# Softmax of 16,384 rows: transfers of 3 to 32 rows per partition in place of transfers of 8

## The chip, the cores and the metric

The kernel runs on one core of a Trainium2 chip. The metric is the device time of one execution, in microseconds (us). The span that the profile shows is about 1.8 us shorter than the device time (161.3 us of span for 163.08 us). All positions in time below are counted from the start of the span. The engines that matter are DVE (VectorE), ACT (ScalarE), SP (SyncE, which only issues the loads) and the core's 16 DMA engines.

With one core, a run is called slow when it is over 1.5% above the fastest of the same kernel, and fast otherwise.

## The reference

```python
# x: 16 x 1024 x 512, float32
x_max = np.max(x, axis=-1, keepdims=True)
exp_x = np.exp(x - x_max)
return exp_x / np.sum(exp_x, axis=-1, keepdims=True)
```

There are 16,384 rows of 512 numbers (2 KB), so each of the 128 partitions gets 128 rows. "One row" below means one row on every partition, which is 262,144 bytes. 33.55 MB come in and 33.55 MB go out.

## The kernel before

The input is cut into 16 chunks of 8 rows. A partition's 8 rows lie next to each other in memory, so one transfer moves 128 pieces of 16 KB. Twelve chunks fit at a time (192 KB per partition). The loads are issued by SP and the stores by ACT's queue.

```python
CHUNKS = [8] * 16
SLOTS = {8: 12}
# ... src[k], dst[k]: chunk k as "(p r) d -> p r d"

    def load(k):
        tiles[k] = data.tile([P, R, d], F32, ..., bufs=SLOTS[R])
        nc.sync.dma_start(out=tiles[k], in_=src[k])
    def rowmax(k):          # DVE, one instruction per chunk
        nc.vector.reduce_max(out=shift[k], in_=tiles[k], axis=AX, negate=True)
    def exps(k):            # ACT, one instruction per row, in place, with the row's sum
        for r in range(R):
            nc.scalar.activation(out=tiles[k][:, r, :], in_=tiles[k][:, r, :],
                                 func=EXP, bias=shift[k][:, r:r+1], ...,
                                 accum_out=sums[k][:, r:r+1])
    def scale(k):           # DVE, in place
        nc.vector.reciprocal(out=recip, in_=sums[k])
        for r in range(R):
            nc.vector.tensor_scalar_mul(out=tiles[k][:, r, :], in0=tiles[k][:, r, :], ...)
    def store(k):
        nc.scalar.dma_start(out=dst[k], in_=tiles[k])

        for k in range(K):
            load(k)
            rowmax(k)
            exps(k)
            if k >= 1:
                scale(k - 1)
                store(k - 1)
        scale(K - 1)
        store(K - 1)
```

Each engine works through its own instructions in this order. DVE's order is therefore: maximum of chunk k, then scaling of chunk k - 1.

Of the kernel before, what the change touches and what calls it, by code (L numbers as in the profile page):

```python
# [1 line left out]

# [4 lines left out]

F32 = mybir.dt.float32
EXP = mybir.ActivationFunctionType.Exp
AX = mybir.AxisListType.X  # L10


CHUNKS = [8] * 16

SLOTS = {8: 12}


@with_exitstack
def kernel(
    ctx: ExitStack,  # L20
    tc: tile.TileContext,
    x: bass.AP,
    out: bass.AP,
):
    nc = tc.nc
    P = nc.NUM_PARTITIONS

    x_flat = x.flatten_outer_dims()
    out_flat = out.flatten_outer_dims()
    n, d = x_flat.shape  # L30
    assert n == P * sum(CHUNKS)


    src, dst, at = [], [], 0
    for R in CHUNKS:
        for flat, views in ((x_flat, src), (out_flat, dst)):
            part = flat[at : at + P * R, :]
            views.append(part.rearrange("(p r) d -> p r d", r=R))
        at += P * R

    data = ctx.enter_context(tc.tile_pool(name="data", bufs=1))
    stats = ctx.enter_context(tc.tile_pool(name="stats", bufs=4))

    K = len(CHUNKS)
    tiles = [None] * K
    shift = [None] * K
    sums = [None] * K

    def load(k):
        R = CHUNKS[k]  # L50
        tiles[k] = data.tile([P, R, d], F32, name=f"x{R}", tag=f"x{R}", bufs=SLOTS[R])
        nc.sync.dma_start(out=tiles[k], in_=src[k])  # L52

    def rowmax(k):
        R = CHUNKS[k]
        shift[k] = stats.tile([P, R], F32, name=f"shift{R}", tag=f"shift{R}")
        nc.vector.reduce_max(out=shift[k], in_=tiles[k], axis=AX, negate=True)  # L57

    def exps(k):
        R = CHUNKS[k]  # L60
        sums[k] = stats.tile([P, R], F32, name=f"sums{R}", tag=f"sums{R}")
        for r in range(R):
            nc.scalar.activation(  # L63
                out=tiles[k][:, r, :],
                in_=tiles[k][:, r, :],
                func=EXP,
                bias=shift[k][:, r : r + 1],
                scale=1.0,
                accum_out=sums[k][:, r : r + 1],
            )  # L70

    def scale(k):
        R = CHUNKS[k]
        recip = stats.tile([P, R], F32, name=f"recip{R}", tag=f"recip{R}")
        nc.vector.reciprocal(out=recip, in_=sums[k])  # L75
        for r in range(R):
            nc.vector.tensor_scalar_mul(  # L77
                out=tiles[k][:, r, :],
                in0=tiles[k][:, r, :],
                scalar1=recip[:, r : r + 1],  # L80
            )

    def store(k):
        nc.scalar.dma_start(out=dst[k], in_=tiles[k])  # L84

    with tc.manual_schedule():
        for k in range(K):
            load(k)
            rowmax(k)
            exps(k)  # L90
            if k >= 1:
                scale(k - 1)
                store(k - 1)
        scale(K - 1)
        store(K - 1)


# [1 line left out]
_INS = ['x']  # L99
_OUTS = [((16, 1024, 512), 'float32')]  # L100


# [23 lines left out]
```

## Time and profile before

| | before |
|---|---|
| device time, median | 163.06 us (162.9 to 163.22) |
| span | 161.3 us |
| DVE busy / ACT busy | 123.8 us / 93.2 us |
| DMA busy, both queues (98.1% of the span) | 158.2 us |
| span less DMA busy | 3.1 us |
| last store issued | 149.49 us |

The lines below are from the page of the kernel before. The rows of DVE and DMA give the busy tenths in 40 slices of the span (about 4 us each). GB/s is what the DMA engines moved. The two queue lines give packets, MB and their time as a share of 16 engines' span (q1 carries the loads, q10 the stores). Then come the chain that ended last, the groups (busy us, mean ns of one, idle time before them) and the transfers (KB each, median us from issue to landing).

```profile
span 161.3 us, 527 instructions
DVE 123.8 (77%) x160; ACT 93.2 (58%) x257; POOL 0.2 (0%) x4
...
DVE  0088799999999999985970079999999999957000
...
DMA  6999999999999999999999999999999999999993
GB/s 163 431 427 427 431 435 378 418 445 431 423 439 431 421 435 431 431 439 418 439 435 427 431 427 435 435 425 435 431 427 439 431 427 427 431 435 431 431 435 171
...
q1 hardware_dynamic: 2304, 33.56, 49.5%
q10 hardware_dynamic: 2304, 33.56, 48.6%
...
DMA 52%; DVE 31%; ACT 6%; SPq 2%; issue 1%; ACTq 1%; DVEq 0%
...
L63 ACT ACTIVATE x<-x,shift 128x512 f32<-128x512 f32 x128 | 90.5, 709 | 44.1 <-DVE shift L57 21.4
L57 DVE TENSOR_REDUCE shift<-x 128x8 f32<-128x4096 f32 x16 | 70.6, 4415 | 9.7 <-DMA x<-in_x_dram 9.7
L77 DVE TENSOR_SCALAR x<-x,recip 128x512 f32<-128x512 f32 x128 | 52.1, 482 | 0.6
...
x<-in_x_dram SPq DMA_DIRECT2D x16, 2048.0 KB, 42.6
out_dram<-x ACTq DMA_DIRECT2D x16, 2048.0 KB, 18.0
```

And from the timeline (start us, us, engine, line, operation), the last store:

```profile
149.49 0.34 ACTq L84 DMA_DIRECT2D out_dram<-x  x1
```

How to read it: the DMA engines are at 90% or more in every slice but the first and the last, at about 431 GB/s, and 49.5% + 48.6% of the span is 158.2 us. DVE and ACT have idle time that costs nothing, because the DMA is the limit. At that rate one row costs the DMA about 0.608 us (262,144 bytes at 431 GB/s), whether it is loaded or stored, so a load or store of 8 rows costs 4.9 us and one of 32 rows 19.5 us. For DVE a row costs 0.97 us: 4415 ns for the maxima of 8, 3.26 us for 8 scalings in the timeline, and a reciprocal.

The rate is what the Trainium skill leads one to expect: "HBM Reference", section "Specifications (TRN2)", says that a core streaming alone measures about 425 GB/s, bounded by its 16 DMA engines. This trace agrees, with 427 to 435 GB/s in most slices.

### The profile page before, as it was taken

What the parts mean: (1) busy time and instruction counts of PE and PEld (TensorE: products, weight loads), DVE (VectorE), ACT (ScalarE), POOL (GpSimd) and SP (SyncE); (2) the same over time, 40 slices, a digit from 0 to 9 for tenths busy, and PEclk for the clock granted to TensorE, in tenths of its full rate; (3) what the DMA queues carried; (4) which work ended last, traced back from release to release, by engine and by line L of the source; (5) the groups of instructions that cost most, each with busy time, mean ns of one, the idle gap of its engine ahead of it and who ended that gap; (6) DMA issues with size and microseconds to landing.
All of it is one profiled execution on the core that took longest, in us unless ns stands there. A gap on an engine that the chain in (4) does not pass through costs nothing.

```text
span 161.3 us, 527 instructions
## 1 busy us (share of the span) xinstructions
DVE 123.8 (77%) x160; ACT 93.2 (58%) x257; POOL 0.2 (0%) x4
## 2 busy tenths in 40 slices
DVE  0088799999999999985970079999999999957000
ACT  0037994959596867067002996859595959591000
POOL 0000000000000000000000000000000000000000
DMA  6999999999999999999999999999999999999993
GB/s 163 431 427 427 431 435 378 418 445 431 423 439 431 421 435 431 431 439 418 439 435 427 431 427 435 435 425 435 431 427 439 431 427 427 431 435 431 431 435 171
DMA packets 4612, 67.14 MB, mean 416 GB/s; under 512 B 513, under 2 KB 513, under 8 KB 513
## 3 DMA queue, kind: packets, MB, share of 16 engines
q1 hardware_dynamic: 2304, 33.56, 49.5%
q10 hardware_dynamic: 2304, 33.56, 48.6%
q14 instruction: 4, 0.02, 0.0%
HBM read 33.55 MB, written 33.55 MB: 416 GB/s over the span
## 4 chain that ended last, share of the span: by engine, by line
DMA 52%; DVE 31%; ACT 6%; SPq 2%; issue 1%; ACTq 1%; DVEq 0%
DMA x<-in_x_dram 52%; DVE shift L57 16%; DVE x L77 14%; ACT x L63 6%; SPq L52 2%; DVE recip L75 1%; ACTq L84 0%; DVEq L121 0%; ACTq L63 0%
## 5 line engine op out<-in xcount | busy, mean ns | idle before, releaser
L63 ACT ACTIVATE x<-x,shift 128x512 f32<-128x512 f32 x128 | 90.5, 709 | 44.1 <-DVE shift L57 21.4
L57 DVE TENSOR_REDUCE shift<-x 128x8 f32<-128x4096 f32 x16 | 70.6, 4415 | 9.7 <-DMA x<-in_x_dram 9.7
L77 DVE TENSOR_SCALAR x<-x,recip 128x512 f32<-128x512 f32 x128 | 52.1, 482 | 0.6
L63 ACT ACTIVATION_READ_ACCUMULATOR x<-x,shift 128x1 f32 x128 | 24.0, 187 | 0.0
L75 DVE RECIPROCAL recip<-sums 128x8 f32<-128x8 f32 x16 | 3.1, 196 | 15.3 <-ACT x L63 15.3
L63 ACT ACT_TABLE_LOAD x1 | 1.3, 1283 | 8.7 <-DMA x<-in_x_dram 8.7
L110 POOL MEMSET const-bfloat16-1.0<- 128x1 bf16 x1 | 0.1, 102 | 0.0
L110 POOL MEMSET const-uint8-127<- 128x1 uint8 x1 | 0.1, 102 | 0.0
L110 POOL MEMSET const-float32-0.0<- 128x1 f32 x1 | 0.1, 99 | 0.2 <-issue 0.2
L110 POOL MEMSET const-float32-1.0<- 128x1 f32 x1 | 0.1, 99 | 0.0
## 6 DMA issues: line engine op xcount, KB each, us to landing
x<-in_x_dram SPq DMA_DIRECT2D x16, 2048.0 KB, 42.6
out_dram<-x ACTq DMA_DIRECT2D x16, 2048.0 KB, 18.0
```

What stands on the lines that cost most here:

```text
L52: nc.sync.dma_start(out=tiles[k], in_=src[k])
L57: nc.vector.reduce_max(out=shift[k], in_=tiles[k], axis=AX, negate=True)
L63: nc.scalar.activation(out=tiles[k][:, r, :], in_=tiles[k][:, r, :], func=EXP, bias=shift[k][:, r : r + 1], scale=1.0, accum_out=sums[k][: ...
L75: nc.vector.reciprocal(out=recip, in_=sums[k])
L77: nc.vector.tensor_scalar_mul(out=tiles[k][:, r, :], in0=tiles[k][:, r, :], scalar1=recip[:, r : r + 1],)
L110: nc = _bacc.Bacc("TRN2", target_bir_lowering=False, num_devices=1)
```

## The change

The intent: one array of 96 rows per partition (192 KB) holds three quarters of the input. The input comes in seven chunks: six that grow (3, 5, 9, 17, 31, 31 rows) and a last one of 32, which goes over the space of the first four. There is one load and one store per chunk. The arithmetic works in groups of about 8 rows, as before. The larger part of the difference:

```diff
-CHUNKS = [8] * 16
-SLOTS = {8: 12}
+CHUNKS = [(3, 0), (5, 3), (9, 8), (17, 17), (31, 34), (31, 65), (32, 0)]   # rows, place
+SBUF_ROWS = 96
+EARLY = 6
+AFTER_STORE = {3: [6]}
+GROUP = 8
...
+    held = data.tile([P, SBUF_ROWS, d], F32, name="held")
+    place = [held[:, s : s + R, :] for R, s in CHUNKS]
+    groups = []
+    for k, (R, _) in enumerate(CHUNKS):
+        m = max(1, round(R / GROUP))
+        cuts = [R * i // m for i in range(m + 1)]
+        groups += [(k, a, b, b == R) for a, b in zip(cuts, cuts[1:])]
...                                    # rowmax, exps: the same on rows a to b of a chunk
+    def scale(g):
+        k, a, b, last = groups[g]
...                                    # reciprocal and scaling of rows a to b
+        if last:
+            nc.scalar.dma_start(out=dst[k], in_=place[k])
+            for later in AFTER_STORE.get(k, ()):
+                load(later)
...
+        for k in range(EARLY):
+            load(k)
+        for g in range(len(groups)):
+            rowmax(g)
+            exps(g)
+            if g >= 1:
+                scale(g - 1)
+        scale(len(groups) - 1)
```

More of the change, by code (lines that the diff above doesn't have):

```diff
@@ L30 @@
     n, d = x_flat.shape
-    assert n == P * sum(CHUNKS)
+    assert n == P * sum(R for R, _ in CHUNKS)
     src, dst, at = [], [], 0
-    for R in CHUNKS:
+    for R, _ in CHUNKS:
         for flat, views in ((x_flat, src), (out_flat, dst)):
@@ L42 @@
     stats = ctx.enter_context(tc.tile_pool(name="stats", bufs=4))
-    K = len(CHUNKS)
-    tiles = [None] * K
-    shift = [None] * K
-    sums = [None] * K
-    def load(k):
-        R = CHUNKS[k]
-        tiles[k] = data.tile([P, R, d], F32, name=f"x{R}", tag=f"x{R}", bufs=SLOTS[R])
-        nc.sync.dma_start(out=tiles[k], in_=src[k])
-    def rowmax(k):
-        R = CHUNKS[k]
-        shift[k] = stats.tile([P, R], F32, name=f"shift{R}", tag=f"shift{R}")
-        nc.vector.reduce_max(out=shift[k], in_=tiles[k], axis=AX, negate=True)
@@ L59, in exps @@
-    def exps(k):
-        R = CHUNKS[k]
-        sums[k] = stats.tile([P, R], F32, name=f"sums{R}", tag=f"sums{R}")
-        for r in range(R):
+    held = data.tile([P, SBUF_ROWS, d], F32, name="held")
[5 more added lines that the diff above has]
+        groups += [(k, a, b, b == R) for a, b in zip(cuts, cuts[1:])]
+    shift = [None] * len(groups)
@@ L63, in exps, with rowmax @@
+    sums = [None] * len(groups)
+    def load(k):
+        nc.sync.dma_start(out=place[k], in_=src[k])
+    def rowmax(g):
+        k, a, b, _ = groups[g]
+        shift[g] = stats.tile([P, b - a], F32, name="shift", tag="shift")
+        nc.vector.reduce_max(
+            out=shift[g], in_=place[k][:, a:b, :], axis=AX, negate=True
+        )
+    def exps(g):
+        k, a, b, _ = groups[g]
+        sums[g] = stats.tile([P, b - a], F32, name="sums", tag="sums")
+        for r in range(a, b):
             nc.scalar.activation(
-                out=tiles[k][:, r, :],
@@ L65, in exps @@
-                in_=tiles[k][:, r, :],
+                out=place[k][:, r, :],
+                in_=place[k][:, r, :],
                 func=EXP,
-                bias=shift[k][:, r : r + 1],
+                bias=shift[g][:, r - a : r - a + 1],
                 scale=1.0,
-                accum_out=sums[k][:, r : r + 1],
+                accum_out=sums[g][:, r - a : r - a + 1],
             )
-    def scale(k):
-        R = CHUNKS[k]
-        recip = stats.tile([P, R], F32, name=f"recip{R}", tag=f"recip{R}")
-        nc.vector.reciprocal(out=recip, in_=sums[k])
-        for r in range(R):
+    def scale(g):
+        k, a, b, last = groups[g]
+        recip = stats.tile([P, b - a], F32, name="recip", tag="recip")
+        nc.vector.reciprocal(out=recip, in_=sums[g])
+        for r in range(a, b):
@@ L77, in scale @@
             nc.vector.tensor_scalar_mul(
-                out=tiles[k][:, r, :],
-                in0=tiles[k][:, r, :],
-                scalar1=recip[:, r : r + 1],
-            )
-    def store(k):
-        nc.scalar.dma_start(out=dst[k], in_=tiles[k])
+                out=place[k][:, r, :],
+                in0=place[k][:, r, :],
+                scalar1=recip[:, r - a : r - a + 1],
+            )
+        if last:
+            nc.scalar.dma_start(out=dst[k], in_=place[k])
+            for later in AFTER_STORE.get(k, ()):
+                load(later)
@@ L86 @@
     with tc.manual_schedule():
-        for k in range(K):
+        for k in range(EARLY):
             load(k)
-            rowmax(k)
-            exps(k)
-            if k >= 1:
-                scale(k - 1)
-                store(k - 1)
-        scale(K - 1)
-        store(K - 1)
+        for g in range(len(groups)):
[4 more added lines that the diff above has]
+        scale(len(groups) - 1)
 _INS = ['x']
```

## The prediction

> **What bounds it now.** The DMA engines. The row of slices shows DMA at 9 in slices 2 to 39, at 418 to 445 GB/s apart from one at 378; 67.14 MB move in about 156 us, between a 2.5 us start and a 2.4 us tail (estimates from the first and last slice). One row per partition (262 KB) costs 0.608 us of DMA time, load or store, and 256 of them 155.7 us. DVE is busy 123.8 us (77%) and ACT 93.2 us: both hide. From the groups and the timeline, one row costs DVE 0.55 us of maximum (4415 ns for 8) and 0.41 us of scaling (3.26 us for 8), with the reciprocal 0.97 us; ACT 0.70 us.
>
> **What the change does.** Bytes, arithmetic and the 192 KB used stay. Only grain changes: 7 loads and stores instead of 16. Few fixed costs vanish, as issues (0.34 us) were hidden: under 1 us. The grain costs in three places:
>
> 1. In the new instruction order the scaling of a chunk's last group stands behind the next chunk's first maximum, which waits for that whole chunk's landing. A store therefore waits for the next load.
> 2. The 32-row load waits for the first four stores; the fourth is issued only after the fifth chunk (31 rows) has landed.
> 3. The last store is 32 rows: it can't start before the last scaling, and takes 19.5 us plus about 4 us of start, landing and end (before: 8 rows, 4.9 us).
>
> **Estimate in order of time** (0.608 us per row, shared when loads and stores compete; 1.35 us from issue to first byte, 1.25 us to landing, estimates from the first load):
> chunk of 17 lands near 26 us; the 31s near 47 to 54 and 70 to 80; the 17-row store is issued at 56 to 62, lands near 83. DMA then idles about 3 us, and the 32-row load runs from 84 to 114-120, beside the first 31-row store (issued 86 to 93). The second 31-row store is issued only near 125 to 130: DMA idle 4 to 9 us. DVE needs 31 us for the last 32 rows, so the last store is issued near 152 to 157, DMA idle about 8 us before it. Span 174 to 181 us, plus 1.8 us (163.08 measured against a span of 161.3).
>
> The width comes from arbitration. The Trainium skill, "DMA: Bandwidth & Descriptors", section "Queues, rings and completion order", says that each DMA engine alternates between queues packet by packet. In the trace a packet is 16 KB on both queues (2304 less 256 small ones, 33.56 MB), so shares were equal. If packets now are as long as a partition's piece (6 to 64 KB), long loads starve short stores at first, DVE gets chunks earlier, but the 31-row store starts sooner and delays the 32-row load: 181. Equal shares: 175. I lean to the former.
>
> **Predicted: 181 us, range 174 to 186; faster 0.01, same 0.04, slower 0.95.**
>
> **What would show it.** DMA slices near zero around 81-84, 123-131 and 147-158 us; DVE busy unchanged, with a wait of 5 to 20 us for the load before the last chunk's first maximum; the chain ending in DVE lines, then a store of over 20 us; about 900 data packets per queue; near 430 GB/s while both queues work.
>
> **What would make it wrong.** Loads taking nearly all bandwidth from stores throughout (DVE hardly stalls, only the final 23 us is exposed: about 165); a higher rate with long packets; packets cut into small pieces (equal shares, 177).

## The result, and the profile after

The changed kernel takes 184.72 us (median of 4, 184.3 to 185.07) against 163.06 us (162.9 to 163.22). The ratio is 1.1327, with a 95% interval of 1.1293 to 1.1361. Here and below, a ratio is the mean time of one kernel's fast runs over that of the other kernel's fast runs of the same rounds, so it is not quite the ratio of the medians quoted.

| | before | after |
|---|---|---|
| device time, median | 163.06 us | 184.72 us |
| span | 161.3 us | 182.5 us |
| DVE busy / ACT busy | 123.8 / 93.2 us | 124.0 / 93.4 us |
| DMA busy, both queues | 98.1%: 158.2 us | 86.9%: 158.6 us |
| span less DMA busy | 3.1 us | 23.9 us |
| last store issued; from there to the end | 149.49; 11.8 us | 160.85; 21.7 us |

The work is the same on every engine. The DMA engines are busy for the same 158 us, and the 21.2 us that the span grew by are 20.8 us more of DMA idle time. Lines of the page of the changed kernel, in the same order as before, with some of the transfers (a slice is 4.6 us; the last line, the 32-row load, is from the fuller list of its DMA transfers):

```profile
span 182.5 us, 502 instructions
...
DVE  0579639992299999999999990008999999520000
...
DMA  6999999998979898987799999990099990095995
GB/s 221 424 453 402 419 476 398 515 471 307 507 329 482 381 480 382 435 374 245 230 452 452 454 452 452 452 417 28 0 445 445 445 445 0 0 431 259 460 460 230
...
q1 hardware_dynamic: 1008, 33.55, 44.3%
q10 hardware_dynamic: 1008, 33.55, 42.6%
...
DMA 62%; DVE 17%; ACT 5%; issue 2%; SPq 1%; DVEq 0%; ACTq 0%
...
L65 DVE TENSOR_REDUCE shift<-held 128x8 f32<-128x4096 f32 (+4 forms) x17 | 70.8, 4163 | 33.7 <-DMA held<-in_x_dram 33.7
...
held<-in_x_dram SPq DMA_DIRECT2D x1, 2304.0 KB, 12.2
out_dram<-held ACTq DMA_DIRECT2D x1, 2304.0 KB, 39.9
held<-in_x_dram SPq DMA_DIRECT2D x1, 1280.0 KB, 7.2
out_dram<-held ACTq DMA_DIRECT2D x1, 1280.0 KB, 33.7
...
held<-in_x_dram SPq DMA_DIRECT2D x1, 39.5
```

The maxima waited 33.7 us for loads, against 9.7 us before. The slices of DMA that were full in before now have holes. The transfers at the bottom show something else: the 5-row store (1280 KB, 3.0 us of data) needed 33.7 us from issue to landing, while long loads were in the other queue. (For the first 11 us of these it stood behind the 3-row store in its own queue; its own packets ran from 32.1 to 52.1 us.) The 5-row load, issued among other loads, needed 7.2 us.

The packet count says how transfers are cut. Of the 1008 packets of a queue, 112 are small ones (16 per transfer), and 896 carry data: 128 per transfer, one for each partition. So a packet is a partition's whole piece, from 6 KB (3 rows) to 64 KB (32 rows).

The single values in the row of GB/s are not to be trusted where packets are long. Values like 515 next to 307 lie in stretches where, over a long window, the mean is 429 (below). The view counts a packet whole where it starts, which is also why some shares below are above 1.00.

Now the timeline of the changed kernel: start us, us, engine, line, operation. These are the starts that matter in the second half, with idle time before an instruction in brackets:

```profile
84.32 0.33 SPq L60 DMA_DIRECT2D held<-in_x_dram  x1
86.66 0.34 ACTq L93 DMA_DIRECT2D out_dram<-held  x1
...
123.84 4.42 DVE L65 TENSOR_REDUCE shift<-held 128x8 f32<-128x4096 f32 x1 [14.41 <-DMA held<-in_x_dram]
...
131.69 0.34 ACTq L93 DMA_DIRECT2D out_dram<-held  x1
...
160.85 0.34 ACTq L93 DMA_DIRECT2D out_dram<-held  x1
```

These are, in order: the 32-row load; the first 31-row store; the first maximum of the last chunk, after 14.4 us of waiting for that load; the second 31-row store; and the 32-row store. The busy share of the DMA in stretches around them (columns: stretch, its length, busy us and instructions of DVE, ACT and POOL, granted clock, DMA share, GB/s):

```profile
4.00:80.00 76.00, 60.38 (x75) 46.23 (x126) 0.00 (x0) 1.00 1.01 429
80.00:88.00 8.00, 7.96 (x11) 6.58 (x19) 0.00 (x0) 1.00 0.59 218
88.00:122.00 34.00, 21.32 (x29) 17.62 (x50) 0.00 (x0) 1.00 1.01 425
122.00:134.00 12.00, 10.13 (x11) 5.66 (x16) 0.00 (x0) 1.00 0.40 169
134.00:150.00 16.00, 15.93 (x21) 11.61 (x33) 0.00 (x0) 1.00 1.03 444
150.00:165.00 15.00, 8.28 (x19) 5.75 (x16) 0.00 (x0) 1.00 0.33 140
```

There are three holes: 3.3 us between 80 and 88, 7.2 us between 122 and 134, and 10.0 us between 150 and 165 (length times one less the share). Counted by the overlap of each packet record in the trace with the stretch, they are 3.2, 7.3 and 10.4 us. In the first, the 32-row load waits for the 17-row store. In the second, the second 31-row store waits for its last scaling, which stands in DVE's order behind the maximum that waited for the 32-row load. In the third, the 32-row store waits for its last group. In between, the rate is as before.

A second way to split the 21.2 us: the last store is issued 11.4 us later (160.85 against 149.49), and takes 9.9 us more from issue to the end of the span (21.7 against 11.8). The experiments attack these two parts separately.

### The profile page after: what moved, and what is told of

It reads as the page before. It is cut to its first block, busy times and chain, and to the rows that moved or that the text cites. A ratio compares the mean times of both kernels' runs of the same rounds, so it can differ in the third digit from the quotient of the medians.

```text
span 182.5 us, 502 instructions
## 1 busy us (share of the span) xinstructions
DVE 124.0 (68%) x162; ACT 93.4 (51%) x257; POOL 0.2 (0%) x4
## 3 DMA queue, kind: packets, MB, share of 16 engines
q1 hardware_dynamic: 1008, 33.55, 44.3%
q10 hardware_dynamic: 1008, 33.55, 42.6%
HBM read 33.55 MB, written 33.55 MB: 368 GB/s over the span
## 4 chain that ended last, share of the span: by engine, by line
DMA 62%; DVE 17%; ACT 5%; issue 2%; SPq 1%; DVEq 0%; ACTq 0%
DMA held<-in_x_dram 47%; DMA out_dram<-held 15%; DVE shift L65 10%; DVE held L87 7%; ACT held L73 5%; SPq L60 1%; DVE recip L85 0%; DVEq L131 0%; ACTq L73 0%
## 5 line engine op out<-in xcount | busy, mean ns | idle before, releaser
L73 ACT ACTIVATE held<-held,shift 128x512 f32<-128x512 f32 x128 | 90.6, 709 | 58.5 <-DVE shift L65 55.1
L65 DVE TENSOR_REDUCE shift<-held 128x8 f32<-128x4096 f32 (+4 forms) x17 | 70.8, 4163 | 33.7 <-DMA held<-in_x_dram 33.7
L87 DVE TENSOR_SCALAR held<-held,recip 128x512 f32<-128x512 f32 x128 | 52.2, 481 | 0.6
L73 ACT ACTIVATION_READ_ACCUMULATOR held<-held,shift 128x1 f32 x128 | 23.9, 187 | 0.0
L85 DVE RECIPROCAL recip<-sums 128x8 f32<-128x8 f32 (+4 forms) x17 | 3.3, 192 | 2.5 <-ACT held L73 2.5
## 6 DMA issues: line engine op xcount, KB each, us to landing
out_dram<-held ACTq DMA_DIRECT2D x1, 1280.0 KB, 33.7
```

The costliest lines, as they stand in the source:

```text
L65: nc.vector.reduce_max(out=shift[g], in_=place[k][:, a:b, :], axis=AX, negate=True)
L73: nc.scalar.activation(out=place[k][:, r, :], in_=place[k][:, r, :], func=EXP, bias=shift[g][:, r - a : r - a + 1], scale=1.0, accum_out=s ...
L85: nc.vector.reciprocal(out=recip, in_=sums[g])
L87: nc.vector.tensor_scalar_mul(out=place[k][:, r, :], in0=place[k][:, r, :], scalar1=recip[:, r - a : r - a + 1],)
```

## The experiments

The theory: nothing is slower, but transfers that are long wait for whole chunks and make others wait, which leaves the DMA without work in three places; and packets of different length share the engines unequally, which decides when the 32-row load lands. The rivals: long transfers or long packets are slow in themselves (the page's mean rate fell from 416 to 368 GB/s); and, for the late 32-row load, that it is late because it is issued late (84.3 us), not because of what runs beside it.

All kernels below are the changed kernel with one edit, and all gave correct results. Each was timed against the kernel before on the same chip, which took 163.07, 163.21 and 163.14 us (medians).

| run | edit | median us | ratio to before | DMA busy, us | span less busy, us |
|---|---|---|---|---|---|
| after | | 184.72 | 1.133 | 158.6 | 23.9 |
| e1 | scaling first at every chunk's end | 180.7 | 1.108 | 158.7 | 20.2 |
| e1b | the same at one chunk's end | 183.04 | 1.122 | 158.5 | 22.9 |
| e2 | last store by groups | 174.38 | 1.070 | 159.1 | 13.7 |
| e3 | last load in pieces | 183.18 (176.09 to 184.53) | none | 157.6 | 16.7 |
| e4 | e2 and e3 (profile of the slow run, 168.92) | 166.65 | 1.020 | 158.2 | 8.9 |
| e5 | first 31-row store in four | 174.2 | 1.066 | 158.5 | 13.8 |
| e11 | e2 and e5 | 166.8 | 1.022 | 159.0 | 6.1 |
| e9 | e4 and e1b | 167.05 | 1.025 | 158.5 | 7.5 |
| e6 | all stores by groups | 163.97 | 1.005 | 158.1 | 3.9 |
| e10 | e6 and e3 | 164.13 | 1.006 | 158.1 | 4.4 |
| e7 | 16 rows everywhere | 162.5 | 0.995 | 157.0 | 4.2 |

The last two columns are of the profiled run: the sum of the two queues' shares times the span, and the rest. The DMA's busy time hardly moves in any run (157.0 to 159.1 us), so the span of each profiled run differs by its idle column.

### e2: the last store alone

```diff
-        if last:
+        if k == 6:
+            nc.scalar.dma_start(out=dst[k][:, a:b, :], in_=place[k][:, a:b, :])
+        elif last:
             nc.scalar.dma_start(out=dst[k], in_=place[k])
...                                    # the issue of the last load stays
```

> Step 3 alone: the last 32 rows are stored in four DMAs of 8 rows, each after its group's scaling. The last scaling should still end near 160.8 us; then 8 rows are left (4.9 us of data) instead of 32 (19.5 us), and the end comes 8 to 14 us sooner: 171 to 177 us. Rival (the transfers themselves are slow when large, and nothing waits on the last one in particular): within 3 us of 184.7.

Measured: 174.38 us (174.18 to 175.07), which is 10.3 us less than after. The last store in its timeline:

```profile
161.28 0.34 ACTq L93 DMA_DIRECT2D out_dram<-held  x1
```

It is issued no earlier than in after, but the span (172.8 us) ends 11.5 us later instead of 21.7. So the exposed store cost about 10 us, and accounts for the second part of the split above. That is less than the 14.6 us that the 24 other rows take (an estimate, at 0.608 us a row): with the second 31-row store issued only at 132.12 us, the DMA still had earlier stores to move. Its share was 1.02 from 140 to 160 us, and 0.96 from 140 us to the end.

### e5: the length of the packets beside the 32-row load

```diff
-        if last:
+        if last and k == 4:
+            for c, d in ((0, 7), (7, 15), (15, 23), (23, 31)):
+                nc.scalar.dma_start(out=dst[k][:, c:d, :], in_=place[k][:, c:d, :])
+        elif last:
             nc.scalar.dma_start(out=dst[k], in_=place[k])
...                                    # the issue of the last load stays
```

> Arbitration alone: the first 31-row store is issued as four DMAs of 7, 8, 8 and 8 rows at the same moment as the one DMA of 31 rows was (near 86.7 us), so its bytes and its start are the same and only its packets are shorter (14 to 16 KB for 62 KB), beside the 32-row load with packets of 64 KB. If the engines take turns packet by packet, the load gets about four fifths of the bandwidth, lands near 108 to 112 us (123.8 in after) and DVE stops waiting for it: 169 to 175 us. If the two queues share by bytes whatever the packet, nothing moves: 184 to 186 us.

Measured: 174.2 us (173.23 to 174.41), 10.5 us less than after. Transfers of this run, and the first maximum of the last chunk in its timeline:

```profile
held<-in_x_dram SPq DMA_DIRECT2D x1, 30.0
...
113.66 4.42 DVE L65 TENSOR_REDUCE shift<-held 128x8 f32<-128x4096 f32 x1 [5.21 <-DMA held<-in_x_dram]
```

The 32-row load, issued at 83.68 us, landed in 30.0 us instead of 39.5, and DVE waited 5.2 us for it instead of 14.4. It landed at 113.7 us, a little after the 108 to 112 us expected. The same rows were stored in the other queue, and the first of the four stores were issued a little earlier than the one store of after (83.17 us against 86.66), before the last scaling (82.40 to 85.66 us) had ended. The last store went out at 150.68 us instead of 160.85: the first part of the split above. So the load was late because of what ran beside it, and how much that cost depended on the packets' length.

The Trainium skill says this in "DMA: Bandwidth & Descriptors", section "Queues, rings and completion order": each engine goes round the queues with work, a packet at a time. This trace agrees, if a packet is what the trace counts as one, a partition's whole piece: the packets of each queue show it directly. Below are packets, MB and share of the engines' time (q1 carries the loads, q10 the stores), first of after from 92 to 120 us, then of e5 from 88 to 112.5 us:

```profile
q1 hardware_dynamic: 96, 6.29, 51.9%
q10 hardware_dynamic: 88, 5.59, 46.0%
...
q1 hardware_dynamic: 128, 8.39, 81.3%
q10 hardware_dynamic: 127, 1.79, 17.0%
```

The two queues sent almost the same number of packets both times (14 of e5's 127 are small ones). In after a load packet of 64 KB took turns with a store packet of 62 KB, so each queue had about half of the time; in e5 it took turns with one of 14 or 16 KB, and the load had four fifths. In these stretches, then, the sharing was one packet for one packet. At four fifths of the bandwidth 32 rows take 24.3 us (an estimate: 32 rows at 0.608 us, divided by 0.8); in e5's packet records the load ran from 88.5 to 112.6 us, 24.1 us, against 85.3 to 121.1 us, 35.8 us, in after. What the expected 108 to 112 us missed is the start: the first packet of the load came 4.8 us after its issue, behind store packets, where in after it came 1.0 us after. Why the queue that starts second has to wait that long stays open.

### e11: both together

```diff
+        if k == 6:                 # as in e2
+            ...
+        elif last and k == 4:      # as in e5
+            ...
```

> e5 and e2 together: the two changes of store length alone, with the waits and all loads of after left in place. Each alone gave about 10 us. If they act on different stretches (the wait for the 32-row load, and the last store), they add up: 163 to 166 us. If they both only buy the same DMA idle time, 170 us or more.

Measured: 166.8 us (166.52 to 166.91), a little above the range expected. The two edits of 10.3 and 10.5 us together gave 17.9 of the 21.7 us that the change had cost in device time. So they act for the most part on different stretches; 6.1 us of DMA idle time remain, against 3.1 in before.

### e6: all stores by groups

```diff
-        if last:
-            nc.scalar.dma_start(out=dst[k], in_=place[k])
+        nc.scalar.dma_start(out=dst[k][:, a:b, :], in_=place[k][:, a:b, :])
+        if last:
             for later in AFTER_STORE.get(k, ()):
```

> All stores cut to one per group of 7 to 9 rows; loads and the array stay as in after. Grain theory: stores no longer wait for a chunk's end, the space for the 32-row load is free earlier, the tail is 8 rows: 162 to 166 us, as before within 2%. Theory of slow long loads: over 170 us.

Measured: 163.97 us (163.74 to 164.11), a ratio of 1.0047 to before (1.0034 to 1.006). The row of the DMA and the 32-row load in its page:

```profile
DMA  5999989897989799889999779699999999999992
...
held<-in_x_dram SPq DMA_DIRECT2D x1, 29.3
```

All loads are as long as in after, the 32-row load is issued at the same time (84.35 us), and it still waits for the 17 rows in its space to be stored. Yet only 0.8 us of the loss is left, and the first hole is gone: the DMA's share between 80 and 88 us is 1.00, against 0.59 in after. So long loads are not slow, and the wait of the 32-row load for its space costs next to nothing when stores are there to keep the DMA busy meanwhile.

### e3 and e4: the last load in pieces

```diff
-AFTER_STORE = {3: [6]}
+PIECES = {0: (0, 3), 1: (3, 8), 2: (8, 17), 3: (17, 32)}
...
-            for later in AFTER_STORE.get(k, ()):
-                load(later)
+            if k in PIECES:
+                c, d = PIECES[k]
+                nc.sync.dma_start(out=place[6][:, c:d, :], in_=src[6][:, c:d, :])
```

> Step 2 alone: the 32-row load is cut in pieces of 3, 5, 9 and 15 rows, each waiting only for the store that frees its own rows. DMA should not idle near 84 us, three of the pieces land before 90 us, DVE waits for the last chunk less than 5 us (14.4 before), the last store is issued near 147 to 150 us: 170 to 174 us. Rival (the load is late because it shares the engines with the 31-row store, not because it is issued late): the same wait of 10 us or more stays, time over 180.

Measured: 176.09, 184.53, 182.98 and 183.38 us. The clock was the same in all four, but they differ by more than 1.5%, so three count as slow and there is no verdict on the ratio. The expectation (170 to 174) was missed. The profile is of the run with 176.09 us, and shows why even that one is late. Its last piece (the first line), and the same piece in e10 (the second):

```profile
held<-in_x_dram SPq DMA_DIRECT2D x1, 3840.0 KB, 44.4
...
held<-in_x_dram SPq DMA_DIRECT2D x1, 3840.0 KB, 21.4
```

The last piece (15 rows, 3840 KB) was issued near 86.7 us, and landed 44.4 us later, beside the 31-row stores. It had become the shorter packet (30 KB beside 62 KB): it had its turns, but each moved less than half of what a store's turn moved. The rival named for this run was right about this piece: cutting the load let the other pieces start earlier (31.14 us for the first), but the last one could start no earlier than the whole load of after (86.75 against 84.32 us), and had a smaller share.

e4 adds e2's edit to it:

> e2 and e3 together. If waits through grain are the whole loss, this is 163 to 167 us, although the loads of 17, 31 and 31 rows and the stores of 17, 31 and 31 rows stay as long as in the changed kernel. If long transfers or long packets run at a lower rate (mean 368 GB/s in the profile of after against 416), it stays above 172.

Measured: 166.65 us; the three fast runs are 165.59 to 166.91, at a ratio of 1.0197 (1.0157 to 1.0237), and one run, the profiled one, took 168.92 and counts as slow. The expected range held for the fast runs. Its loads of up to 31 rows, and stores of up to 31 rows, speak against slow long transfers as e6 does.

### e10: pieces, with short stores beside them

```diff
+PIECES = {0: (0, 3), 1: (3, 8), 2: (8, 17), 3: (17, 32)}     # as in e3
+        nc.scalar.dma_start(out=dst[k][:, a:b, :], in_=place[k][:, a:b, :])   # as in e6
```

> e3's load pieces with all stores cut to 7 to 9 rows. In e3 the last load piece (15 rows, packets of 30 KB) took 44 us to land beside stores with packets of 62 KB, and its runs spread from 176 to 184.5 us. If that is short packets losing turns to long ones, the piece now lands in under 30 us and the runs agree within 1 us, at 162 to 165 us. If the pieces are slow for another reason (their number, or their waits), the landing stays at 40 us and the spread stays.

Measured: 164.13 us (163.72 to 164.26). The piece landed in 21.4 us (the line above), and the spread of e3 is gone. Compared with e6 the pieces gain nothing: 163.97 and 164.13 us, each against before on its own chip, are ratios of 1.0047 and 1.0058. So it was the long stores that made e3 late; this run also issues them at other times, so it does not separate the length of their packets from their timing. Why e3's four runs differ among themselves by 8 us can't be read from one profile, and stays open.

### e1, e1b and e9: the order at the end of a chunk

This tests step 1 of the prediction: the last group's scaling, and so the store, stands behind the next chunk's first maximum.

```diff
         for g in range(len(groups)):
+            early = g >= 1 and groups[g - 1][3]        # e1b, e9: and groups[g - 1][0] == 5
+            if early:
+                scale(g - 1)
             rowmax(g)
             exps(g)
-            if g >= 1:
+            if g >= 1 and not early:
                 scale(g - 1)
```

> Step 1 of the prediction alone: at every chunk boundary the last group's scaling is put in front of the next chunk's first maximum, so no store waits for the next chunk's load. If that coupling is a main cost, the 31-row store that was issued at 131.7 us goes out near 121 us and the time falls by 5 us or more, below 180 us. My estimate: DVE now waits for ACT's exponentials at each boundary (about 6 us each time, where it had the next maximum to do), so what is won is given back and the time stays at 183 to 186 us. A rival that blames slow large transfers expects no change.

Measured: 180.7 us (180.68 to 180.74), 4.0 us less than after. My estimate of no gain was wrong, and so was the "5 us or more" of the other theory. The second 31-row store was issued at 122.13 us instead of 131.69, as that theory had said. The waits of e1:

```profile
DVE recip L85 <- ACT held L73: 27.0, 11, 6.5
...
DVE shift L65 <- DMA held<-in_x_dram: 5.2, 1, 5.2
```

DVE's waits for loads fell from 33.7 to 5.2 us, and its waits for ACT rose from 2.5 to 27.0 us: with the scaling in front, DVE has to wait for the exponentials of the same group. Most of what was won was given back.

> e1 (scaling first at every boundary) came out at 180.7 us where I had expected 183 to 186: a miss. Here only the boundary in front of the last chunk is turned. If e1's gain is just that DVE scales 8 rows (3.3 us) while it waits for the 32-row load instead of after it, the same 180 to 182 us come from this one boundary, with the second 31-row store issued near 121 us. If e1's gain came from the earlier boundaries, this stays at 184 to 185 us.

Measured: 183.04 us (182.58 to 183.32), 1.7 us less than after. The store was issued at 115.58 us, 16 us earlier, and only 1.7 us came of it, because the end depends on the last chunk's load, which landed when it had before (DVE started on it at 124.50). The remaining 2.3 us of e1 came with the earlier ends of chunks; there the 32-row load took 37.4 us to land instead of 39.5. What each of them gave was not separated.

> e4 and, in addition, the last scaling of the sixth chunk put in front of the last chunk's first maximum. Estimate 162 to 165 us, 1 to 3 us under e4 if the DVE still sets the end there; equal to e4 if the DMA does.

Measured: 167.05 us (167.01 to 167.74), no better than e4: a miss. The last load piece took 49.9 us to land in it, so the order at the chunk's end was not the limit.

### e7: long transfers everywhere, of one length

```diff
-CHUNKS = [(3, 0), (5, 3), (9, 8), (17, 17), (31, 34), (31, 65), (32, 0)]
+CHUNKS = [(16, 16 * (k % 6)) for k in range(8)]
-AFTER_STORE = {3: [6]}
+AFTER_STORE = {0: [6], 1: [7]}
```

> Transfers of 16 rows throughout (4 MB, packets of 32 KB), six places in the same array, groups of 8. It asks what packet length does to the rate where nothing has to wait. If long packets carry about 450 GB/s, as some slices of the profile of after show, 156 to 159 us. If the rate is that of before plus a packet's fixed cost saved (under 1%), 161 to 163 us. If long transfers are slow, over 168 us.

Measured: 162.5 us (162.29 to 162.95), a ratio of 0.9953 (0.9939 to 0.9966): half a per cent faster than before, and the fastest version. Its row of the DMA and its queues:

```profile
DMA  7999999999999999999999999999999999999993
...
q1 hardware_dynamic: 1152, 33.55, 49.1%
q10 hardware_dynamic: 1152, 33.55, 48.3%
```

The DMA is as full as in before, although DVE waits 20.0 us for loads here (9.7 before). Its busy time is 157.0 us, against 158.2, with packets of 32 KB instead of 16. So packets twice as long are worth about 1 us, not the 452 or 460 GB/s that some slices of the profile of after seem to show. Those come from how the view counts. The packet records of the traces say so directly: the median packet took 611 ns for 16 KB (before), 1213 ns for 32 KB (e7) and 2342 ns for 62 KB (after), which for 16 engines is 429, 432 and 434 GB/s. This settles the first rival: long packets are not slow in themselves.

## Why the prediction was right

The prediction said 181 us, with a range of 174 to 186; measured were 184.72 us.

- "The DMA engines" bound the kernel before, and the change leaves the DMA's work alone: shown. DMA busy was 158.2 us before and 158.6 after, and 157.0 to 159.1 in every experiment.
- "Under 1 us" of gain from fewer transfers: e7, with half the transfers of before and no hole in the DMA's row, gained 0.7 us between medians.
- Three idle stretches of "about 3", "4 to 9" and "about 8" us: measured 3.3, 7.2 and 10.0 us, near the places named (each ended about 2 to 4 us later than named).
- "A wait of 5 to 20 us for the load before the last chunk's first maximum": 14.4 us. "About 900 data packets per queue": 896. Near 430 GB/s while both queues work: 429 between 4 and 80 us, 425 between 88 and 122.
- The last store "takes 19.5 us plus about 4": measured 21.7 us from issue to end, 1.8 us less than that sum; e2 showed that cutting it is worth 10.3 us.
- Arbitration: the prediction leaned to shares by packet length (181) over equal shares (175). e5 shows that packet length matters, and after itself shows it: between 32 and 50 us 108 load packets of 62 KB and 125 store packets of 10 KB were sent, 6.86 MB against 1.28. Beside the 32-row load, where packets were 64 and 62 KB, both rules give about equal shares; what the leaning rested on there is that the 31-row store would start soon, and it was issued at 86.66 us, early in the range of 86 to 93.

What was off:

- The estimate was 3.7 us too low. The term that was mis-sized is the landing of the 32-row load: "114-120" predicted, 123.8 measured. The load took 39.5 us where 30 to 36 were allowed: 1.0 us to its first packet, 35.8 us for its packets (of the 128, all but the first 32 shared the engines with the store), and 2.7 us until DVE started. Its small last packets came up to 2.3 us after its data, which is about one packet of the store (2.34 us). With it everything behind it came later: the second 31-row store at 131.7 (predicted 125 to 130) and the last store at 160.85 (152 to 157).
- Step 1, the order at the end of a chunk, stood beside the other two as if of the same kind. On its own it is worth 4.0 us at most (e1), because the scaling has to wait for ACT if it doesn't wait for the load.
- Step 2, the wait of the 32-row load for its space, is real (84.3 us) but isn't what costs: in e6 it waits as long, and the time is within 0.5% of before. The cost is that the DMA had no other work in the hole, and that the load then shared the engines with packets as long as its own.

What stays open: why the queue that starts second waits about 5 us for its first packet, the spread of e3, and how e1's gain divides over the ends of chunks.

## What to carry to other kernels

When a kernel is bound by the DMA, compare the DMA's busy time with the span: a change of grain leaves the first alone, and everything it costs or gains is in the difference. Here long loads that were issued early were harmless (e6). Stores of 31 and 32 rows were not (e5, e2), because each waits for all of its rows, the last one is exposed when the DMA has nothing else to do, and a long packet takes bandwidth from whatever the compute engines are waiting for. Stores of 16 rows, with loads of the same length beside them, cost nothing (e7), so it is not length alone that counts but whether the DMA has other work meanwhile. If two transfers run side by side and one is waited for, let that one have the longer packets, and end the kernel on a short store if the DMA would otherwise run dry before it.

## What the Trainium skill lacked or had wrong

- "DMA: Bandwidth & Descriptors", section "SWDGE vs HWDGE vs iDMA", gives a packet as at most 4096 bytes preferably, and as the boundary for switching, for the descriptors that GpSimd writes; for loads and stores from SP and ACT no page read gives a packet's size. Here the trace has one packet per partition's piece, of 6 to 64 KB (896 data packets for 33.55 MB per queue), and the queues took turns at that grain.
- The same page, section "Queues, rings and completion order", says that the engines go round the queues packet by packet, but not what follows: a queue's share depends on its packets' length. Packets went nearly one for one (96 and 88 in after, 128 and 127 in e5), so the 32-row load landed in 39.5 us beside 62 KB packets and in 30.0 us beside packets of 14 to 16 KB.
- No page read says what packets beyond 16 KB are worth: 32 KB gave 157.0 us of DMA time against 158.2 for the same bytes (1213 ns a packet against 611), and a ratio of 0.9953.
- No page read warns that rates by slices mislead with long packets: slices of 452 to 515 GB/s appear in a stretch whose mean over a long window is 425 to 429.
